# An encoder layer in split float32: the down projection's weights at other byte shifts, in longer tiles

## The chip, the cores and the metric

The kernel runs on one core of one Trainium2 chip. The time is the device time of one execution in microseconds; a kernel's time is the median of its runs. The engines are named as in the profile: PE (TensorE; PEld are its weight loads), ACT (ScalarE), DVE (VectorE), POOL (GpSimd) and SP (SyncE, which here only issues DMAs).

## The reference

One layer over 1024 rows of 1024 float32: pooling and differential attention, merged by gates, then the multi-layer perceptron whose last product is the down projection:

```python
def reference(x, ...):
    ...
    x = x + merged @ w_out[l]
    h2 = rmsnorm(x, g_ffn[l])
    x = x + jnp.square(jax.nn.relu(h2 @ w_up[l])) @ w_down[l]
    return x
```

`h2` is 1024 x 1024, `w_up` 1024 x 4096, `w_down` 4096 x 1024.

## The kernel before

**Digits.** Every float32 operand of a product is split in two: `hi`, a rounded copy of the value, which ACT casts (line 131), and `lo`, what is left, which DVE (or POOL) subtracts (line 132). A product `a b` is then three matmuls into one PSUM bank, `hi hi`, `hi lo` and `lo hi` (`mm3`, lines 137 to 139). In the matmuls of the down projection the stationary operand, which TensorE loads as weights, is a 128 x 128 block of `uh` or `ul` (activation sums), and the moving one is 128 x 512 of `wh` or `wl` (rows of `w_down` or sums of its quarters).

**The up and the down projection** each take seven products of halves instead of eight, by the scheme of Strassen and Winograd. The up projection runs over 16 pairs of column blocks (`up_pair`, p = 0 to 15). Each pair's results and four sums of them are stored to DRAM (`ud`, `udS`), 8 tiles of 128 x 2 x 512 for each of seven names.

**The down projection** runs over the products `"1"`, `"2"`, `"6"`, `"5"`, `"7"`, `"3"`, `"4"` (`d_product`), and in each over `q` = 0 to 7: 56 pairs (j, q). For a pair, `operands(j, q)` loads the raw activation sums `ur` from DRAM (line 1370) and the raw quarter `wd` of `w_down` (line 1333), or makes a sum of quarters on DVE (`T1s`, `T2s`), and splits both. `d_step` then makes 2 x 4 x 3 matmuls into the four banks of the product (`Da` or `Db`; `i` is the half of the tile, `t` the bank). A tile's name has product and pair, as `u1_0h`: product 1, pair 0, hi; the profile's rows leave the product out (`u_0h`). While product 1 runs, `wdt` quarters are loaded as well, for the sums `T1s` (`t1_made`). `x1y` and the like are the results of a product plus the rows of the residual (`with_residual`).

**Buffers.** The pools of this stage lie on the right side of SBUF one behind the other, in the order `pur0` (2 raw tiles for `ur`), `prw0` (2 for `wd`), `puo` (8 tiles for `u` digits, so that four pairs' digits exist at a time), `pur1` (2), `prw1` (4); `pwo`, 8 tiles for `w` digits, lies on the left. They lie where buffers of the up projection lay (`pr1`, `pr20`, `pr21` for raw `w_up`, `e20`, `e21`, `es` for sums), and a tile may be written once the readers of what lay there before are done.

**The order** of instructions on each engine is set by a scheduler when the program is built. It goes by priorities in the order of the code, and by its own estimate of when things are ready; the first three pairs of product 1 are given the priority of the up projection's last pair (`early`), so that their loads and splits mix with it. Each engine's queue runs in order. SP's queue holds the loads of both raw operands, so a load that waits for a buffer holds up all behind it.

Of the kernel before, what the change touches and what calls it, by code (L numbers as in the profile page):

```python
# [9 lines left out]
F32R = mybir.dt.float32r  # L10
# [7 lines left out]
P = 128  # L18
# [37 lines left out]
}  # L56
O_TAIL = "a0 70 n0 71 n1 72 n2 40 s0 n3 73 41 s1 42 t0 s2 43 t1 s3"
A_ROOM = {"1": 1, "2": 0, "6": 1, "5": 0, "3": 1, "7": 0, "4": 1}

N_OP, N_E1, N_E2, N_R1, N_R2 = 8, 11, 6, 4, 3  # L60

# [2 lines left out]
def encoder_kernel(  # L64
# [22 lines left out]
    x, out = x[0], out[0]  # L87
# [41 lines left out]
    def split(hi, lo, src, lo_eng=None):  # L129

        nc.scalar.copy(hi, src)  # L131
        return (lo_eng or nc.vector).tensor_tensor(lo, src, f(hi), op=ALU.subtract)  # L132
# [281 lines left out]
    with ExitStack() as ph:  # L414
# [364 lines left out]
        for g in range(-2, N + 10):  # L779
# [11 lines left out]
            for tok in ORDER:  # L791
                if tok not in gens:
                    i = g - tok[1]
# [66 lines left out]
    for d in range(NK):  # L860
        if d % 2 == 0 and d + 2 < NK:
            ws_bp[d + 2] = load_cols2(w_branch_pool, (d + 2) * P, f"bp{d + 2}")
        elif d > NK - 4:
            j = len(ws_ba)
# [12 lines left out]
    def a_set(j, d):  # L877

        t = hp0[A_ROOM[j]].tile([P, 2, 512], F32R, tag="H", name=f"A{j}_{d}")
        a_sets.setdefault(j, []).append(t)  # L880
# [455 lines left out]
    def second(j, q):  # L1336

        if j == "1":
            b11[q] = quarter(j, q, 0, 0)
            return b11[q]  # L1340
        if j == "5":
            return T1s[q]
        if j == "2":
            return quarter(j, q, 1, 0)
        if j == "3":
            return quarter(j, q, 1, 1)
        if j == "6":
            b22 = quarter(j, q, 1, 1)
            T2s[q] = kept("T2", q)
            sub(dve, T2s[q], b22, T1s[q])  # L1350
            return T2s[q]
        if j == "7":
            b22, b12 = quarter(j, q, 1, 1), quarter(j, q, 0, 1)
            sub(dve, b22, b22, b12)
            return b22
        b21 = quarter(j, q, 1, 0)
        sub(dve, b21, b21, T2s[q])
        return b21
# [8 lines left out]
    def operands(j, q):  # L1367
        nraw[0] += 1
        ur = purs[nraw[0] > 2 and nraw[0] % 2].tile([P, 2, 512], F32, tag="ur", name=f"ur{j}_{q}")
        nc.sync.dma_start(ur, ud[SIDES[j][0], q])  # L1370
        out_ = []
        for n, src, pool_ in (("u", ur, puo), ("w", second(j, q), pwo)):
            hi, lo = (pool_.tile([P, 2, 512], F32R, tag="op", name=f"{n}{j}_{q}{x}") for x in "hl")
            split(hi, lo, src, dve)
            out_ += [hi, lo]
        return out_
# [11 lines left out]
    def d_product(banks, j, last=False, early={}):  # L1388
        for q in range(NQ - 2 if last else NQ):
            d_step(banks, j, q, early.get(q) or operands(j, q), range(4))  # L1390
            if j == "1" and q > 1:
                t1_made(q - 2)
        if j == "1":
            t1_made(NQ - 2)
            t1_made(NQ - 1)
        if last:
            ops = {q: operands(j, q) for q in (NQ - 2, NQ - 1)}
            for t in range(4):
                for q in ops:
                    d_step(banks, j, q, ops[q], (t,))  # L1400
# [23 lines left out]

    now, tc.cur_priority = tc.cur_priority, last_pair
    early = {q: operands("1", q) for q in range(3)}
    tc.cur_priority = now
    DX = four("a")
# [49 lines left out]
```

## Time and profile before

| | |
|---|---|
| median of 3 runs (lowest, highest) | 1532.88 us (1532.23, 1533.74) |
| the profiled execution | 1532.49 us; its span, first to last instruction, 1530.7 us |
| busy, share of the span: PE, PEld, DVE, ACT, POOL | 99%, 86%, 67%, 52%, 25% |
| granted TensorE clock | 1.00 |
| chain that ended last | PE 97%, DVE 2% |
| down projection | from 1221.7 us on, about 309 us |

PE's busy share counts matmuls that overlap each other in the pipeline, so the distance from one start to the next is the better measure of its rate. A row of a timeline has start and length in us, engine, line, operation, tiles, and in brackets the idle time before it and what ended it. A row of a tile has duration in ns (least, median, most) and the first and last start in us.

### The profile page before, as it was taken

To read this page: it belongs to the slowest core of one execution; us is meant where nothing else is said; L and a number is where in the kernel's file an instruction comes from. 1 tells how busy PE (TensorE), PEld (TensorE's weight loads), DVE (VectorE), ACT (ScalarE), POOL (GpSimd) and SP (SyncE) were. 2 spreads that over 40 slices of the span, in tenths; PEclk is the share of its full clock that TensorE was granted. 3 is DMA by queue.
4 is the path that set the end of the run, shared out by engine and by line. 5 is a ranking of instruction groups with operands and counts; after the bars stand their busy time and mean duration, and the time that the engine had idled before them with its cause. 6 is when DMAs were issued, how large, how long until landed. Compare 5 with 4: busy or idle time off the path is not lost.

```text
span 1530.7 us, 21680 instructions
## 1 busy us (share of the span) xinstructions
PE 1513.4 (99%) x7601; PEld 1314.4 (86%) x7601; DVE 1027.9 (67%) x2129; ACT 794.7 (52%) x1650; POOL 390.1 (25%) x469
## 2 busy tenths in 40 slices
PE   7999999999999999999999999999999999999999
PEld 6999999999999999888888887888888788888887
DVE  7777766677777777743654899676656678556572
ACT  5656555555555565544633467565555634333331
POOL 5434242433435352317736610000000000000000
PEclk9999999999999999999999999999999999999999
DMA  7111111111202021329844633555433889537650
GB/s 226 42 58 60 46 56 56 50 56 34 76 33 80 31 90 49 114 99 365 279 148 164 210 149 117 172 186 166 151 124 110 288 322 369 188 124 261 228 192 28
DMA packets 168569, 214.28 MB, mean 140 GB/s; under 512 B 10158, under 2 KB 104075, under 8 KB 168459
## 3 DMA queue, kind: packets, MB, share of 16 engines
q1 hardware_dynamic: 151050, 185.58, 35.8%
q10 hardware_dynamic: 17408, 27.30, 4.9%
q8 instruction: 60, 0.98, 0.3%
q14 instruction: 51, 0.41, 0.1%
HBM read 155.14 MB, written 57.70 MB: 139 GB/s over the span
## 4 chain that ended last, share of the span: by engine, by line
PE 97%; DVE 2%; DMA 0%; issue 0%; ACT 0%; SPq 0%; POOL 0%; ACTq 0%; POOLq 0%
PE z L139 6%; PE z L137 6%; PE z L138 6%; PE g L139 4%; PE g L138 4%; PE g L137 4%; PE Da L138 4%; PE Da L139 4%; PE Da L137 4%; PE Db L137 3%; PE Db L139 3%; PE Db L138 3%; PE X L139 3%; PE X L137 3%; PE X L138 3%; PE sc L630 2%
## 5 line engine op out<-in xcount | busy, mean ns | idle before, releaser
L137 PE MATMUL z<-wqkv,hT 128*128 128x384 f32 x512 | 175.5, 343 | 0.0
L139 PE MATMUL z<-wqkv,hT 128*128 128x384 f32 x512 | 174.3, 341 | 0.7 <-DVE hT L132 0.7
L138 PE MATMUL z<-wqkv,hT 128*128 128x384 f32 x512 | 174.7, 341 | 0.0
L641 ACT ACTIVATE s<-s,nm 128x256 f32<-128x256 f32 (+7 forms) x128 | 99.6, 778 | 74.3 <-DVE nm L633 71.5
L270 POOL TENSOR_TENSOR ms<-ms,mhalf 128x4 f32<-128x4 f32 x64 | 65.1, 1017 | 207.7 <-DVE ms L269 196.5
L137 PE MATMUL g<-hT,fwgate 128*128 128x512 f32 x256 | 101.1, 395 | 0.0
L139 PE MATMUL g<-hT,fwgate 128*128 128x512 f32 x256 | 100.6, 393 | 0.0
L138 PE MATMUL g<-hT,fwgate 128*128 128x512 f32 x256 | 100.5, 393 | 0.0
L137 PEld LDWEIGHTS z<-wqkv,hT 128*128 128x128 f32 x512 | 97.3, 190 | 2.6 <-ACT hT L131 0.4
L139 PEld LDWEIGHTS z<-wqkv,hT 128*128 128x128 f32 x512 | 97.1, 190 | 2.7 <-DVE hT L132 1.5
L138 PEld LDWEIGHTS z<-wqkv,hT 128*128 128x128 f32 x512 | 97.4, 190 | 1.7
L633 DVE CUSTOM_DVE_ANT_0 s<-sc,dist 128x512 f32<-128x512 f32 (+3 forms) x128 | 74.3, 585 | 23.3 <-PE sc L631 22.3
L630 PE MATMUL sc<-K,Q 128*128 128x512 f32 (+2 forms) x192 | 67.2, 355 | 0.4 <-DVE nm L633 0.4
L631 PE MATMUL sc<-K,Q 128*128 128x512 f32 (+2 forms) x192 | 66.3, 349 | 0.0
L132 POOL TENSOR_TENSOR wqkv<-rqkv,wqkv 128x384 fp32r<-128x384 f32 x60 | 62.4, 1055 | 12.9 <-ACT wqkv L131 8.1
L132 DVE TENSOR_TENSOR AS<-s,AS 128x512 fp32r<-128x512 f32 x64 | 43.5, 689 | 32.9 <-ACT AS L131 32.8
L132 POOL TENSOR_TENSOR fwgate<-frgate,fwgate 128x512 fp32r<-128x512 f32 x32 | 44.1, 1378 | 63.5 <-ACT fwgate L131 63.5
L139 PEld LDWEIGHTS g<-hT,fwgate 128*128 128x128 f32 x256 | 48.1, 188 | 9.6
L137 PEld LDWEIGHTS g<-hT,fwgate 128*128 128x128 f32 x256 | 48.2, 188 | 9.0 <-ACT go L388 0.2
L138 PEld LDWEIGHTS g<-hT,fwgate 128*128 128x128 f32 x256 | 48.2, 188 | 8.6 <-issue 0.2
L137 PE MATMUL ba<-yT,wba 128*128 128x512 f32 x128 | 49.7, 389 | 0.0
L139 PE MATMUL ba<-yT,wba 128*128 128x512 f32 x128 | 49.7, 389 | 0.0
(458 smaller groups left out, 4597.9 us busy)
## 6 DMA issues: line engine op xcount, KB each, us to landing
wd<-in_w_down_dram SPq DMA_DIRECT2D x56, 512.0 KB, 5.5
wu<-in_w_up_dram SPq DMA_DIRECT2D x32, 512.0 KB, 4.9
udS<-us SPq DMA_DIRECT2D x64, 256.0 KB, 3.5
ur<-udS SPq DMA_DIRECT2D x32, 512.0 KB, 3.2
rqkv<-in_w_in_dram SPq DMA_DIRECT2D x64, 192.0 KB, 2.8
ur<-ud SPq DMA_DIRECT2D x24, 512.0 KB, 5.4
frgate<-in_w_gate_dram SPq DMA_DIRECT2D x32, 256.0 KB, 2.7
g_dram<-go ACTq DMA_DIRECT2D x32, 256.0 KB, 2.9
```

What stands on the lines that cost most here:

```text
L132: return (lo_eng or nc.vector).tensor_tensor(lo, src, f(hi), op=ALU.subtract)
L137: nc.tensor.matmul(ps, lhs_hi, rhs_hi, start=first, stop=False, **kw)
L138: nc.tensor.matmul(ps, lhs_hi, rhs_lo, start=False, stop=False, **kw)
L139: return nc.tensor.matmul(ps, lhs_lo, rhs_hi, start=False, stop=last, **kw)
L270: nc.gpsimd.tensor_tensor(dst, dst, mhalf[:, :n], op=ALU.pow)
L630: nc.tensor.matmul(dst, Q[:, i, 0, :], rhs, start=True, stop=False)
L631: nc.tensor.matmul(dst, Q[:, i, 1, :], rhs, start=False, stop=True)
L633: nc.vector.tensor_tensor_reduce(out=s[i][:, c : c + w], in0=sc[:, 0:w], in1=dist[:, o0 + c : o0 + c + w], scale=2.0 ** -(h + 1), scalar=B ...
L641: nc.scalar.activation(s[i][:, 0:n], s[i][:, 0:n], AF.Exp, bias=last, scale=-1.0, accum_out=Z[:, i, t : t + 1])
```

## The change

The `u` tiles of the down projection become 64 floats longer, 1088 in place of 1024 for each partition, and the digits lie `o` floats (4 `o` bytes) behind the tile's start. `o` comes from a table with an entry for each pair (j, q), the same for `hi` and `lo`; products are counted as 1 to 7 in it. It has 24 different values: the multiples of 4 from 0 to 60 three times each, and 1, 2, 3, 5, 6, 7, 62 and 63 once each. The `w` tiles stay as they are. So ACT's cast writes, DVE's subtraction reads and writes, and TensorE's weight loads read at shifted addresses; no instruction is added or left out.

```diff
+SHIFT = [4, 56, 40, 12, 16, 0, 32, 24, 40, 28, 12, 52, 24, 48, 44, 16, 63, 6, 60, 60, 4, 8, 20, 8, 20, 48, 5, 28, 40, 52, 44, 4, 1, 36, 36, 52, 36, 7, 44, 48, 56, 12, 0, 2, 0, 3, 16, 62, 32, 56, 24, 28, 32, 8, 20, 60]
...
         for n, src, pool_ in (("u", ur, puo), ("w", second(j, q), pwo)):
-            hi, lo = (pool_.tile([P, 2, 512], F32R, tag="op", name=f"{n}{j}_{q}{x}") for x in "hl")
+            if n == "u":
+                o = SHIFT[8 * (int(j) - 1) + q]
+                hi, lo = (
+                    pool_.tile([P, 2 * 512 + 64], F32R, tag="op", name=f"{n}{j}_{q}{x}")[:, o : o + 2 * 512]
+                    .rearrange("p (i c) -> p i c", i=2)
+                    for x in "hl"
+                )
+            else:
+                hi, lo = (pool_.tile([P, 2, 512], F32R, tag="op", name=f"{n}{j}_{q}{x}") for x in "hl")
             split(hi, lo, src, dve)
```

The 8 tiles of `puo` take 8 x 256 = 2048 bytes of each partition more, and `pur1` and `prw1` behind them lie 2048 bytes lower. Which buffers of the up projection they overlap changes with that, and with it what the first tiles wait for; the scheduler's order changes between the up projection's last pairs and the first pairs of product 6. Ahead of it and from there on the order on every engine is the one of before, but for two operations of DVE that change places in product 6. Lines below the table are numbered 2 higher, those below `operands` 10 higher. Three places of the order are shown in the prediction.

## Prediction

> **What bounds the kernel now.** I read the page's first part and its chain first, then stretches of the down projection, then single rows.
>
> ```profile
> span 1530.7 us, 21680 instructions
> PE 1513.4 (99%) x7601; PEld 1314.4 (86%) x7601; DVE 1027.9 (67%) x2129; ACT 794.7 (52%) x1650; POOL 390.1 (25%) x469
> PE 97%; DVE 2%; DMA 0%; issue 0%; ACT 0%; SPq 0%; POOL 0%; ACTq 0%; POOLq 0%
> 1222.00:1232.00 10.00, 9.87 (x44) 7.83 (x43) 8.74 (x10) 6.13 (x9) 0.00 (x0) 1.00 0.54 205
> 1232.00:1264.00 32.00, 32.00 (x143) 26.51 (x142) 20.67 (x19) 11.59 (x12) 0.00 (x0) 1.00 0.96 350
> 1264.00:1306.00 42.00, 42.00 (x187) 34.80 (x186) 34.53 (x32) 17.83 (x18) 0.00 (x0) 1.00 0.99 370
> 1306.00:1530.00 224.00, 221.03 (x976) 182.77 (x974) 122.22 (x118) 74.06 (x74) 0.00 (x0) 1.00 0.48 166
> ```
>
> TensorE (PE) is the bound: 97% of the chain that ended last. The last four rows cut the down projection into stretches (length, then busy time and count of PE, of the weight loads, of DVE, ACT and POOL, then granted clock, DMA share, GB/s). From 1222 us on PE is busy all through, at a granted clock of 1.00, and only between 1232 and 1306 us is a second resource near its limit: the DMA engines at 0.96 and 0.99. So the change can move the end in two ways: by the time from one matmul to the next in this stage, or by a wait of PE for digits (the hi and lo parts that ACT and DVE make).
>
> **The change, first part: weights at other addresses.** Each of the 56 pairs feeds 2 x 4 x 3 = 24 matmuls, 1344 in all. Three entries of the table are 0, so 53 pairs, 1272 matmuls, get weights from a new address modulo 256 bytes. In the built program of before every matmul operand of this width starts at a multiple of 256 bytes. What a load and a matmul take there:
>
> ```profile
> L137 PEld LDWEIGHTS Da<-w_2h,u_2h x32: 187/188/188, 1232.9 to 1498.8; 128*128 128x128 f32 x32
> L137 PE MATMUL Da<-w_2h,u_2h x32: 388/390/390, 1233.1 to 1499.0; 128*128 128x512 f32 x32
> ```
>
> ```profile
> 1224.72 0.39 PE L139 MATMUL Da<-w_0h,u_0l 128*128 128x512 f32 x1
> ...
> 1227.44 0.39 PE L139 MATMUL Da<-w_0h,u_0l 128*128 128x512 f32 x1
> ...
> 673.86 0.28 PE L138 MATMUL po<-AT_0l,V 128*128 128x256 f32 x1
> ...
> 676.49 0.28 PE L139 MATMUL po<-AT_4h,V 128*128 128x256 f32 x1
> ```
>
> The first two rows give min/median/max in ns. The timeline rows give starts: 12 steps between the first two, 2.72 / 12 = 227 ns for a matmul of 512 columns; 22 steps between the last two, 2.63 / 22 = 120 ns for 256 columns. The 256 columns more cost 107 ns, so 512 columns alone take 214 ns and some 13 ns are left that do not depend on the width. A load shows 188 ns, yet the matmuls of 256 columns, each with a load of its own, come every 120 ns: loads are pipelined, and beside 227 ns at least 107 ns of a load's part stay unused. A load could therefore become longer by some 100 ns before PE felt it. I take 0 for the loads. The bounds come from below and above: the 13 ns could vanish, -1272 x 13 ns = -16.5 us; for a loss the nearest rows are matmuls of the same width that are longer in other stages:
>
> ```profile
> L137 PE MATMUL g<-hT,fwgate 128*128 128x512 f32 x256 | 101.1, 395 | 0.0
> L630 PE MATMUL sc<-K,Q 128*128 128x512 f32 x96 | 39.1, 407 | 0.4 <-DVE nm L633 0.4
> L137 PE MATMUL Da<-w_2h,u_2h 128*128 128x512 f32 x32 | 12.5, 389 | 0.0
> ```
>
> They are 6 and 18 ns above 389: +7.6 and +22.9 us. The value taken is 0 because the row nearest by place, the load itself, has that slack.
>
> [...]
>
> The casts on ACT (1.05 us) and the subtractions on DVE (1.23 us) that write the digits at the new addresses lie beside PE. In the steady part a digit of u is ready 14 to 15 us before its use (u_4h below: cast at 1227.64, used from 1244.0), so a cast that took twice as long would cost nothing; without that cover it would be 1.05 us for a pair.
>
> **Second part: the pools move.** The eight u tiles grow by 256 bytes each, so that the raw buffers behind them lie 2048 bytes lower and the first u tile overlaps a raw buffer of the up projection's last pair (p = 15). The first u digit now waits until DVE has read that buffer. On ACT, around the last pair, before (u1_0h is the first digit of product 1's pair 0):
>
> ```order
> L131 CAST AS4_14_12663<-s4_14_12582 128x512
> L131 CAST u1_0h_12852<-ur1_0_12848 128x1024
> L1233 COPY z5_14_12618<-Z14_12602 128x512
> L131 CAST AS2_15_12699<-s2_15_12694 128x512
> L131 CAST u1_1h_12864<-ur1_1_12860 128x1024
> ```
>
> and in the changed program:
>
> ```order
> L1208 ACTIVATE U2_14_12600<-U2_14_12600 128x512
> L1213 DMA ud12_7_10148<-U3_14_12636 128x512
> L133 CAST u1_0h_12852<-ur1_0_12848 128x1024
> L1209 ACTIVATE U2_14_12600<-U2_14_12600 128x512
> L133 CAST AS4_15_12777<-s4_15_12696 128x512
> L133 CAST u1_1h_12864<-ur1_1_12860 128x1024
> L1230 COPY U2_15_12714<-X15_12539 128x512
> ```
>
> The two casts have moved back past some dozen instructions, into the time just ahead of the down projection, whose start now looks so:
>
> ```profile
> 1197.65 1.05 ACT L131 CAST u_0h<-ur 128x1024 fp32r<-128x1024 f32 x1
> 1209.50 0.63 ACT L1207 ACTIVATE U<-U 128x512 f32<-128x512 f32 x1
> 1215.98 1.05 ACT L131 CAST u_2h<-ur 128x1024 fp32r<-128x1024 f32 x1 [2.08 <-DMA ur<-ud]
> 1218.40 0.59 ACT L1237 COPY U<-X 128x512 f32<-128x512 f32 x1 [0.42 <-PE X L139]
> 1220.60 1.03 ACT L131 CAST w_0h<-wd 128x1024 fp32r<-128x1024 f32 x1
> 1218.21 1.22 DVE L132 TENSOR_TENSOR u_3l<-ur,u_3h 128x1024 fp32r<-128x1024 f32 x1
> 1221.12 0.69 DVE L807 TENSOR_TENSOR U<-Z,U 128x512 f32<-128x512 f32 x1 [0.50 <-PE Z L139]
> 1221.73 1.22 DVE L132 TENSOR_TENSOR w_0l<-wd,w_0h 128x1024 fp32r<-128x1024 f32 x1
> 1200.52 3.22 SPq L1370 DMA_DIRECT2D ur<-ud  x2
> 1221.68 1.20 PE L137 MATMUL Da<-w_0h,u_0h 128*128 128x512 f32 x4 [0.59 <-ACT w_0h L131]
> 1223.00 0.50 PE L138 MATMUL Da<-w_0l,u_0h 128*128 128x512 f32 x1
> ```
>
> Worked through with these durations: u_0h starts at about 1209.5, where Square stood, and ends at 1210.55; u_0l follows on DVE until 1211.8. The load of ur for pair 3 waits for it, so it goes out at 1211.8 and not at 1200.52, and the one for pair 2 lands behind it: u_2h starts at about 1217.3 and not at 1215.98. In the new order u_2h, the copy of U (PE ends X at 1218.40), u_3h (to 1219.95) and two activations stand ahead of w_0h, which ends at 1222.55 and not at 1221.63; DVE does u_3l after two additions, then U, then w_0l, until 1223.95 and not 1222.95. PE's first matmul moves from 1221.68 to 1222.6 and its first with w_0l from 1223.00 to 1223.95: **+1.0 us**. If pair 2 lands as early as now it is +0.3; one more microsecond of landing makes it +2.2.
>
> From there SP's queue, which issues in order, changes too. Before (ur2 belongs to product 2, wd1 to product 1):
>
> ```order
> L1370 DMA ur2_0_13192<-ud12_0_10141 128x1024
> L1333 DMA wd1_4_00_13006<-in_w_down_dram 128x2x512
> L1333 DMA wdt_2_01_13040<-in_w_down_dram 128x2x512
> L1333 DMA wd1_5_00_13046<-in_w_down_dram 128x2x512
> L1333 DMA wdt_3_01_13080<-in_w_down_dram 128x2x512
> L1370 DMA ur2_1_13228<-ud12_1_10142 128x1024
> ```
>
> and after:
>
> ```order
> L1372 DMA ur2_1_13228<-ud12_1_10142 128x1024
> L1335 DMA wd1_4_00_13006<-in_w_down_dram 128x2x512
> L1335 DMA wdt_2_01_13040<-in_w_down_dram 128x2x512
> L1335 DMA wd1_5_00_13046<-in_w_down_dram 128x2x512
> L1335 DMA wdt_3_01_13080<-in_w_down_dram 128x2x512
> L1372 DMA ur2_2_13264<-ud12_2_10143 128x1024
> ```
>
> The load for w_4 now stands behind ur2_1, which waits for DVE's u_5l, and it needs T of pair 0, which DVE does after u_5l:
>
> ```profile
> 1232.50 0.38 SPq L1333 DMA_DIRECT2D wd<-in_w_down_dram  x1
> 1235.43 0.34 SPq L1370 DMA_DIRECT2D ur<-ud  x1
> 1234.17 1.23 DVE L132 TENSOR_TENSOR u_5l<-ur,u_5h 128x1024 fp32r<-128x1024 f32 x1 [0.57 <-ACT u_5h L131]
> 1238.48 1.05 ACT L131 CAST w_4h<-wd 128x1024 fp32r<-128x1024 f32 x1 [4.34 <-DMA wd<-in_w_down_dram]
> 1239.56 1.23 DVE L132 TENSOR_TENSOR w_4l<-wd,w_4h 128x1024 fp32r<-128x1024 f32 x1 [4.17 <-ACT w_4h L131]
> 1227.64 1.05 ACT L131 CAST u_4h<-ur 128x1024 fp32r<-128x1024 f32 x1 [0.57 <-PE Da L138]
> L137 PE MATMUL Da<-w_4h,u_4h x8: 389/390/390, 1244.0 to 1248.8; 128*128 128x512 f32 x8
> 1263.83 1.23 DVE L132 TENSOR_TENSOR w_0l<-wd,w_0h 128x1024 fp32r<-128x1024 f32 x1 [1.24 <-ACT w_0h L131]
> 1264.98 1.28 DVE L807 TENSOR_TENSOR x1y<-Da,x1y 128x512 f32<-128x512 f32 x2
> L138 PE MATMUL Db<-w_0l,u_0h x24: 388/390/390, 1266.7 to 1444.8; 128*128 128x512 f32 x24
> ```
>
> u_5l ends at 1235.4 and T at 1236.6, so w_4's load goes out at 1236.6 and not at 1232.50, 4.1 us later against PE. Today w_4l is done at 1240.8 and needed at about 1244.7: 3.9 us of slack. The load now has one transfer ahead of it and not a full queue, so I expect it after some 4 us and not after the 6.0 us of today (1232.50 to 1238.48): no wait, 0 us (to +0.2 if it takes as long as today). At product 2 there is less: w_0l ends at 1265.1 and is needed at 1266.7, 1.6 us. In DVE's new order three additions x1y stand ahead of w_0l, and the third needs the third bank of product 1, which PE ends 3 x 227 ns = 0.7 us before the product's end. Addition 0.69 and w_0l 1.23 give a w_0l at 1.35 us after that end; PE has 4 x 227 ns = 0.9 us of matmuls that need only w_0h: **+0.5 us** (0 to +2). Later pairs have 4 us and more.
>
> **Sum.** The profiled execution took 1532.49 us, 1.8 us more than its span; +1.0 +0.5 +0 gives 1534.0. The median of the three runs is 0.4 us above that execution: 1534.4 us.
>
> **Rivals.**
> - *Loads from shifted addresses lengthen each matmul (slower).* For it: no row of before tests such an address, and 13 ns per matmul stay unexplained beside the columns. Against it: the 107 ns of slack. Price: 6 ns, as in the gate's matmuls, +7.6 us: 1542.0 us. It decides from 1.2 ns a matmul (1.6 us) on.
> - *Shifted addresses free part of the 13 ns (faster).* For it: that remainder is on the path of every matmul. Against it: it is the same 13 ns at both widths, as a fixed step would be. Half of it: -1272 x 6.5 ns = -8.3 us, 1526.1 us; all of it: 1517.9. [...]
> - *w_0 of product 2 comes late (slower).* The DMA engines are 0.96 busy from 1232 to 1264 us, so 4.1 us lost at the queue may stay lost, and in the new order one more u transfer (512 KB, 1.4 us at 370 GB/s) stands ahead of it. w_0h has 1266.7 - 0.9 - 1263.8 = 2.0 us. Price 4.1 + 1.4 - 2.0 = 3.5 us in place of 0.5: 1537.4 us. It decides once the load is over 2 us late.
>
> **How the numbers follow.** A measurement of this kernel can tell about 0.2%, 3.1 us. The forecast (1533.2 to 1535.9, within that bound) gets 0.45, longer matmuls 0.27, because the new addresses are untested, shorter ones 0.15, late digits 0.13. So faster 0.15, same 0.45, slower 0.27 + 0.13 = 0.40. The range runs from 1526.0, half of the 13 ns freed, to 1542.5, just over the gate's 6 ns; left out are the fuller half of the gain (0.07) and a loss above 6 ns (0.12).
>
> **What would show it.** Right: steps of 227 ns in the down projection for all shifts, loads near 188 ns, PE's first Da matmul about 1 us later, an idle of some 0.5 us before the first w_0l of product 2, and no other. Wrong: steps that differ from pair to pair with the shift, in either direction, or an idle of PE of over 2 us around 1244 or 1267 us.

## The result and the profile after

The changed kernel took 1544.81 us (median of three runs, 1542.64 to 1548.02) against 1532.88 us: a ratio of 1.0080, interval 1.0050 to 1.0109. The forecast was 1534.4 us, its range ended at 1542.5. The profiled execution took 1544.81 us, 12.3 us more than that of before.

The page of after, busy time by engine and the chain by engine:

```profile
span 1543.0 us, 21684 instructions
PE 1519.7 (98%) x7601; PEld 1312.8 (85%) x7601; DVE 1023.4 (66%) x2129; ACT 793.9 (51%) x1650; POOL 391.3 (25%) x469
PE 93%; DVE 2%; DMA 2%; ACT 1%; SPq 1%; issue 1%; POOL 0%; ACTq 0%; DVEq 0%; POOLq 0%
```

PE is still the bound, but ACT, SP's queue and a DMA now stand in the chain: PE waits somewhere. PE has 6.3 us more busy time for the same 7601 matmuls, and the weight loads have no more than before (1312.8 against 1314.4 us): the matmuls became longer.

Where PE waits, by the timeline of after (start, duration, engine, what; idle before it and its releaser). The first three rows are PE's last matmul of the up projection, its first of the down projection and its first of product 2; the last is the cast that the third waits for:

```profile
1220.72 0.39 PE L141 MATMUL Z<-B22h,AS 128*128 128x512 f32 x1
1224.17 1.20 PE L139 MATMUL Da<-w_0h,u_0h 128*128 128x512 f32 x4 [3.07 <-ACT w_0h L133]
1271.66 1.19 PE L139 MATMUL Db<-w_0h,u_0h 128*128 128x512 f32 x4 [2.26 <-ACT w_0h L133]
1270.57 1.04 ACT L133 CAST w_0h<-wd 128x1024 fp32r<-128x1024 f32 x1 [5.92 <-DMA wd<-in_w_down_dram]
```

Before, PE's idle time at the start was 0.59 us and the first Da matmul stood at 1221.68: the start is 2.5 us late. At product 2 there was no wait; now 2.66 us lie between its first matmul and the one before (1269.01, below), where a step is 0.23: 2.4 us.

The same 200 us out of the steady part, before and then after (length, busy time and count of PE, of the loads, of DVE, ACT and POOL, granted clock, DMA share, GB/s):

```profile
1300.00:1500.00 200.00, 200.00 (x884) 165.70 (x883) 118.79 (x113) 72.79 (x74) 0.00 (x0) 1.00 0.55 192
```

```profile
1300.00:1500.00 200.00, 200.00 (x866) 162.17 (x865) 120.55 (x115) 72.01 (x72) 0.00 (x0) 1.00 0.62 205
```

PE is busy all through, at the same clock, with 866 matmuls where there were 884: 200 / 884 = 226 ns for a step, 200 / 866 = 231 ns. Single rows of after, in a pair whose shift is 24, and the group of w_2h, u_2h (min/median/max ns):

```profile
1267.60 0.40 PE L141 MATMUL Da<-w_7h,u_7l 128*128 128x512 f32 x1
...
1269.01 0.40 PE L141 MATMUL Da<-w_7h,u_7l 128*128 128x512 f32 x1
L139 PEld LDWEIGHTS Da<-w_2h,u_2h x32: 187/188/192, 1235.6 to 1510.4; 128*128 128x128 f32 x32
L139 PE MATMUL Da<-w_2h,u_2h x32: 388/394/400, 1235.8 to 1510.6; 128*128 128x512 f32 x32
```

Six steps in 1.41 us are 235 ns. The load keeps its 188 ns (192 at most), the matmul beside it takes 394 ns where it took 390.

The account of the two profiled executions: the down projection starts 2.5 us later, PE waits 2.4 us at product 2, and the rest of the projection grows from 304.96 to 314.77 - 2.43 = 312.34 us between first and last matmul, 7.4 us over the 1272 matmuls with shifted weights or **5.8 ns each**. 2.5 + 2.4 + 7.4 = 12.3 us, the whole difference.

By shift (4-byte elements), the mean steps worked out from the starts: 227.3 ns for 0, 226.7 for 3, 226.8 for 63, 227.9 for 60; 230 to 232 for 1, 2, 6, 20, 44, 48, 52; 233 to 235 for the thirteen others. So it is not the shift's size, and not whether it is a multiple of four. One shift does not always have one price either: of the three pairs shifted by 48, two take 229.3 ns and one 233.3 through all its 24 matmuls; why is not known.

### The profile page after: what moved, and what is told of

It is laid out like the page before. It is cut to its first block, busy times and chain, and to the rows that moved or that the text cites. A ratio compares the mean times of both kernels' runs of the same rounds, so it can differ in the third digit from the quotient of the medians.

```text
span 1543.0 us, 21684 instructions
## 1 busy us (share of the span) xinstructions
PE 1519.7 (98%) x7601; PEld 1312.8 (85%) x7601; DVE 1023.4 (66%) x2129; ACT 793.9 (51%) x1650; POOL 391.3 (25%) x469
## 4 chain that ended last, share of the span: by engine, by line
PE 93%; DVE 2%; DMA 2%; ACT 1%; SPq 1%; issue 1%; POOL 0%; ACTq 0%; DVEq 0%; POOLq 0%
PE z L141 6%; PE z L139 6%; PE z L140 6%; PE g L141 4%; PE g L140 4%; PE g L139 4%; PE Da L140 3%; PE Da L141 3%; PE Da L139 3%; PE Db L140 3%; PE Db L141 3%; PE Db L139 3%; PE X L141 3%; PE X L139 3%; PE X L140 3%; PE sc L632 2%
```

## The experiments

Behind each time stand its ratio to the kernel before, measured beside it (1532.1 to 1533.5 us), and the 95% interval of the ratio.

**Waits and longer matmuls apart.** The long tiles and moved pools alone:

```diff
-SHIFT = [4, 56, 40, 12, ...
+SHIFT = [0] * 56
```

> The long tiles and the moved pools stay, every entry of the table is 0. Theory (two separate costs: late digits from the moved pools, and longer matmuls from the shifted weights): the late start (2.5 us) and the wait at product 2 (2.4 us) stay and all matmul steps of the down projection are 227 ns, so 1532.9 + 4.9 = about 1537.8 us. Rival (the shifts make the waits, or the 4352-byte stride of the tiles lengthens the matmuls): 1533 us in the first case, about 1545 us with steps of 232 ns in the second.

1539.66 us (1.0042, 1.0030 to 1.0054), with 884 matmuls in the 200 us. The order and both waits are those of the changed kernel (idle of 2.23 us at the start and 2.48 us at product 2), the steps are back at 227 ns. So the waits do not come from the shifts, nor the longer steps from the tiles' stride. It is 1.9 us above the expected 1537.8, and the windows of this run show a cost that nobody had expected:

```profile
1222.00:1224.40 2.40, 1.83 (x7) 1.20 (x8) 1.71 (x2) 2.40 (x5) 0.00 (x0) 0.98 0.77 237
1224.40:1228.00 3.60, 3.60 (x11) 2.82 (x10) 3.30 (x4) 2.97 (x5) 0.00 (x0) 0.54 0.59 208
1228.00:1267.90 39.90, 39.90 (x177) 33.01 (x176) 24.99 (x24) 11.28 (x11) 0.00 (x0) 1.00 0.85 293
1267.90:1270.80 2.90, 0.42 (x3) 0.03 (x1) 1.85 (x5) 1.13 (x2) 0.00 (x0) 1.00 1.05 399
1270.80:1272.60 1.80, 1.74 (x5) 1.12 (x6) 1.80 (x2) 1.80 (x3) 0.00 (x0) 0.86 1.06 414
1272.60:1276.00 3.40, 3.40 (x10) 2.69 (x9) 3.40 (x4) 1.91 (x3) 0.00 (x0) 0.57 1.03 388
```

The granted clock falls to half 1.8 us after the end of the first wait and 1.3 us after that of the second, for 3.4 us each time: seven or eight steps of 427 ns, about 1.6 us. (The rows show a little more than 0.5 because their stretches reach beyond it.) The changed kernel's profiled run had no such stretch in spite of its two waits.

The other way round, all shifts but the order of before: the lowest of the eight places of u, which overlaps the raw buffer of the up projection's last pair, is used only for the last digit of every fourth pair.

```diff
-    puo = pool_of(ctx, "puo", 8, side="right")
+    puo = pool_of(ctx, "puo", 7, side="right")
+    pul = pool_of(ctx, "pul", 1, side="right")
...
-    pool_.tile([P, 2 * 512 + 64], ...
+    (pul if q % 4 == 3 and x == "l" else pool_).tile([P, 2 * 512 + 64], ...
```

> All shifts as in the change; the lowest of the eight places, which overlaps the raw buffer of the last pair, is kept for the last digit of every fourth pair, so that the first digit need not wait, and the instructions stand as before but for four loads on SP's queue. Theory of two separate costs: the waits go, the longer steps stay (mean 232.5 ns in the shifted pairs), 1344 x 5.2 ns = 7 us, about 1540 us. Rival (the longer steps only come with the late, crowded order, through the DMA traffic beside them): steps of 227 ns, about 1533 us.

1542.62 us (1.0058, 1.0046 to 1.0070), 865 matmuls in the 200 us. The wait at product 2 is gone: it came from the order that the late first digit brought. (The five other kernels with this order do not have it either, and the run without shifts, with the changed kernel's order, does.) The longer steps stayed. The start was still late (1.85 us of idle), and some 1.6 us went to one stretch at half clock behind it (3.30 us at a granted 0.51). The same kernel with all shifts 0:

> Long tiles, all shifts 0, the lowest place of u kept for the last digit of every fourth pair, the raw buffers of w_down as in the change: the run with the shifts and this layout, without its shifts. Theory (the two costs add: in this layout no wait at product 2 and a start about 1.2 us late, as that run showed; the rest of its time came from the shifts): steps of 227 ns, about 1534 us, and 7 to 8 us below the run with the shifts. Rival (the longer tiles cost by themselves, by the clock or the DMA traffic): 1537 us or more.

1535.06 us (1.0011, 1.0001 to 1.0021), 884 matmuls. Of the 9.2 us of the run before, 7 come from the shifts.

The late start that remains points to a second overlap. The raw buffers of w_down lie behind those of u and move down too; in the built program the buffer of w_down's pair 2 lies over an s tile of pair 15, where before it lay over tiles of pair 14 alone. Two loads on SP's queue, the second of which is this one, and u_2h's cast on ACT, before and then after:

```profile
1195.48 3.41 SPq L1333 DMA_DIRECT2D wd<-in_w_down_dram  x2
```

```profile
1195.49 6.13 SPq L1335 DMA_DIRECT2D wd<-in_w_down_dram  x2
1219.02 1.05 ACT L133 CAST u_2h<-ur 128x1024 fp32r<-128x1024 f32 x1 [4.21 <-DMA ur<-ud]
```

The second load goes out 2.7 us later and SP holds what stands behind it. u_2h's cast starts at 1219.02 and not at 1215.98, but in the changed kernel that load of w_down is not what holds it up. SP's queue further on, before and then after:

```profile
1211.62 0.82 SPq L1370 DMA_DIRECT2D ur<-ud  x2
```

```profile
1203.04 0.47 SPq L1335 DMA_DIRECT2D wdt<-in_w_down_dram  x1
1211.75 0.34 SPq L1372 DMA_DIRECT2D ur<-ud  x1
1212.36 0.34 SPq L1213 DMA_DIRECT2D udS<-us  x1
1212.75 0.94 SPq L1372 DMA_DIRECT2D ur<-ud  x2
```

The loads of ur for pairs 2 and 4 are the last row each time. In after, the load for pair 3 (1211.75) stands ahead of them and waits until u_0l is done; SP had issued nothing for 8 us by then, so the 2.7 us were over. Pair 2's load leaves at 1212.75 where it left at 1211.62, and lands after 6.3 us where it took 4.3. In the run with the lowest place last it leaves in time, but still takes 5.9 us to land.

To take both overlaps away (all shifts 0):

```diff
-    prws.append(pool_of(ctx, "prw1", 4, side="right"))
+    prws.append(pool_of(ctx, "prw1", 3, side="right"))
+    prws.append(pool_of(ctx, "prw2", 1, side="right"))
...
-        r = prws[0 if first else 1].tile(...
+        nraw[2] += not first
+        r = prws[0 if first else 1 + (nraw[2] % 4 == 0)].tile(...
```

> Long tiles, all shifts 0, and both pools that moved (the digits of u, and the raw buffers of w_down below them) use their lowest place for every fourth tile only, so that neither the first digit of u nor the load of w for pair 2 waits for the last pair of the up projection. Theory (the late start and the wait at product 2 come from these two overlaps): the first Da matmul starts about 1 us after the last matmul of the up projection, as before, PE does not wait at product 2, about 1533.5 us. Rival (something else in the longer tiles costs, such as the DMA traffic or the clock): still 1537 us or more.

1537.29 us (1.0030, 1.0020 to 1.0041): half right. PE's first Da matmul:

```profile
1223.99 1.20 PE L139 MATMUL Da<-w_0h,u_0h 128*128 128x512 f32 x4 [0.90 <-ACT w_0h L133]
```

(The up projection itself ended 2.0 us later in this execution than in that of before, so the start is to be read by the idle time.) With both overlaps gone the idle time is 0.90 us here and 0.78 to 1.20 in three more kernels with these places, against 1.55 to 2.93 in six with the first alone removed. So the second overlap has a part in the late start of those six; what it adds in the changed kernel, which has both, was not separated. But PE waits 3 us at product 2: this arrangement changes the order of the w loads of product 1, and w_0 of product 2 comes late again. Which load costs it there was not separated, and it is not the order alone: of the three other kernels with these places and this order two wait there as well (2.7 and 2.0 us), and the one with only the lo digits shifted does not.

**What makes a matmul longer.** With the lowest place last and the weights u at multiples of 256 bytes, the moving operand w shifted by the table:

```diff
-            if n == "u":
-                o = SHIFT[8 * (int(j) - 1) + q]
+            o = SHIFT[8 * (int(j) - 1) + q] if n == "w" else 0
```

> Order as in the run with the lowest place last; the weights u lie at multiples of 256 bytes, and the moving operands w are shifted by the same table in long tiles. Theory A (what counts is where the weights lie): steps of 227 ns everywhere, about 1533 us. Theory B (what counts is the distance between weights and moving operand, modulo 256 bytes): steps near 233 ns in the shifted pairs, about 1540 us. Theory C (any operand off a multiple of 256 bytes costs by itself): also longer, but with other numbers per shift, 1536 to 1545 us.

1541.19 us (1.0051, 1.0039 to 1.0063), 863 matmuls in the 200 us. Weights at their old alignment, and the steps are as long: theory A is out. Then both by the same entry (the condition dropped):

> Order as in the run with the lowest place last; weights and moving operand of a pair are shifted by the same entry of the table. Theory A (weights alone): as with the weights alone shifted, steps near 232.5 ns, about 1540 us. Theory B (distance of the two): back to 227 ns in all pairs, about 1533 us. Theory C (each costs by itself): longer than either alone, 1543 to 1550 us.

1540.44 us (1.0048, 1.0036 to 1.0061), 870 matmuls. None of the three as stated: pairs whose shift is a multiple of 8 elements are back at 227 to 229 ns, odd multiples of 4 stay at 231 to 233. So the distance counts, and something finer beside it. 56 combinations of two shifts in one kernel:

> 56 different pairs of shifts (weights a, moving operand b), in 4-byte elements. Theory B (only the distance a - b modulo 64 elements counts where both are multiples of 8): (64,0), (0,64) and (64,64) take 227 ns; (16,0), (24,8), (32,16), (48,32), (40,24) and (0,48) agree within 1 ns near 233; (48,0), (56,8), (0,16), (8,24), (16,32) agree near 229 to 231. Theory C (each operand costs by its own address): (24,8) and the like differ from (16,0) and come nearer to the sum of two costs, 239 ns.

The kernel took 1545.25 us in one run; its steps are what it was made for. First and last matmul of three of its pairs, with shifts of weights and moving operand of (16,0), (40,24) and (64,0):

```profile
1339.57 0.39 PE L140 MATMUL Da<-w_4h,u_4h 128*128 128x512 f32 x1
...
1344.93 0.39 PE L142 MATMUL Da<-w_4h,u_4l 128*128 128x512 f32 x1
...
1484.15 0.40 PE L140 MATMUL Db<-w_6h,u_6h 128*128 128x512 f32 x1
...
1489.53 0.39 PE L142 MATMUL Db<-w_6h,u_6l 128*128 128x512 f32 x1
...
1423.13 0.39 PE L140 MATMUL Da<-w_3h,u_3h 128*128 128x512 f32 x1
...
1428.36 0.39 PE L142 MATMUL Da<-w_3h,u_3l 128*128 128x512 f32 x1
```

23 steps each: 5.36 / 23 = 233 ns, 5.38 / 23 = 234 ns, 5.23 / 23 = 227 ns. From all starts, for shifts that are multiples of 8 (a - b modulo 64 elements, which are 256 bytes):

| distance | mean step of its pairs, ns |
|---|---|
| 16: (16,0) (24,8) (32,16) (40,24) (48,32) (0,48) | 233.2 232.8 233.8 233.6 232.8 233.0 |
| 32: (32,0) (40,8) (48,16) (16,48) (0,32) | 233.3 232.7 232.4 233.3 232.3 |
| 48: (48,0) (56,8) (0,16) (8,24) (16,32) | 229.3 230.1 229.4 229.8 228.9 |

Theory B holds to about 1 ns, at distances 8, 24 and 56 too (233, 234 and 233 ns); (64,0), (0,64) and (64,64) take 227.3 to 228.6. The shift of 48 in the changed kernel, 229.3 or 233.3 ns, shows that a distance can still have two prices. Where both are odd multiples of 4 the distances have other prices: (20,4) and (28,12), 16 apart, take 229 ns, (12,4) and (20,12), 8 apart, 227 to 228. As a test on whole kernels, both shifted by multiples of 8, at distance 0 and at distance 32:

```diff
+SHIFT = [o // 8 * 8 for o in SHIFT]
...
-            o = SHIFT[8 * (int(j) - 1) + q]
+            o = (SHIFT[8 * (int(j) - 1) + q] + 32 * (n == "w")) % 64
```

The first line alone makes the kernel at distance 0, both make the other.

> The same layout; weights and moving operand of each pair both shifted by the table's entry rounded down to a multiple of 8 elements, so that their distance modulo 64 elements is 0. Theory (the step goes by the distance): 227 to 228 ns, 1534 to 1535 us, as without shifts. Rival (each shift costs by itself): 1540 us and more.

> As the run with equal shifts, but the moving operand 32 elements further (modulo 64), so that the distance is 32 elements in all 56 pairs; tiles, order and the set of addresses are the same. Theory: 232 to 233.5 ns in all 1344 steps, 1344 x 5.8 ns = 7.8 us above the run with equal shifts, about 1542 us. Rival (it is the addresses and not their distance): the same time as that run.

The 200 us at distance 0, then at distance 32:

```profile
1300.00:1500.00 200.00, 200.00 (x880) 164.79 (x879) 119.73 (x114) 73.71 (x74) 0.00 (x0) 1.00 0.58 198
```

```profile
1300.00:1500.00 200.00, 200.00 (x862) 161.82 (x861) 118.72 (x113) 71.03 (x73) 0.00 (x0) 1.00 0.60 202
```

1536.80 us (1.0022, 1.0014 to 1.0031) and 1543.82 us (1.0066, 1.0051 to 1.0082): 7.0 us between two kernels with the same tiles, order and shifts of u, by the distance alone; the mean steps of the two traces, 228.0 and 232.5 ns, make 6.1 us of it. Both lie 2 us above the expected values, the first also 1.7 us above the kernel without shifts. By the starts, steps 10 to 23 of a pair take 226 to 227 ns, the last one, beside which the next pair's weights load from another shift, 231 to 232, and the first nine 228 to 231.

The 53 changes of pair in this trace tell where the price is paid. The first two rows are the last matmul of a pair and the tenth of the next, where the shift goes from 40 to 16; the other two are the same places where it stays at 24:

```profile
1306.73 0.40 PE L142 MATMUL Db<-w_6h,u_6l 128*128 128x512 f32 x1
...
1309.05 0.39 PE L140 MATMUL Db<-w_7h,u_7h 128*128 128x512 f32 x1
...
1416.07 0.39 PE L142 MATMUL Da<-w_2h,u_2l 128*128 128x512 f32 x1
...
1418.33 0.39 PE L140 MATMUL Da<-w_3h,u_3h 128*128 128x512 f32 x1
```

Ten steps take 2.32 us in the first case and 2.26 in the second. At the seven changes to an equal shift nothing happens; at the 46 others the steps around the change are longer, and the sum depends on the distance between the new shift and the old one alone, to 1 ns: 34 ns together at distance 8, 42 at 16, 49 at 24, 10 at 32, 51 at 40, 12 at 48 and 32 at 56. All changes together make 1.5 us of the 1.7. Each matmul's own weights lie at distance 0 from its moving operand here, so the price is paid where a load lies at another distance from the operand that streams just then, and it fades over some ten steps. An earlier run of equal shifts, in the layout with two low places:

> Weights and moving operand of each pair are shifted by the same entry, rounded down to a multiple of 8 elements (32 bytes). Theory B with the parity seen before (equal shifts cost nothing if they are multiples of 32 bytes): all steps near 227 ns and, the places being those of the unshifted run with two low places, about 1533.5 to 1534.5 us. Rival (any shift costs, equal or not): steps of 230 ns and more, 1538 us.

1537.62 us (1.0032, 1.0019 to 1.0046): the steps took 228 ns too, and the time was missed by that layout's 2 us at product 2. Last, only the lo digits of u shifted:

> Only the lo digit of u is shifted by the table; hi digits and w lie at multiples of 256 bytes. Three matmuls follow each other: hi x w hi, hi x w lo, lo x w hi. Theory L (the load of shifted weights gets in the way of the matmul that runs beside it): the step of hi x w lo, beside which the lo digit is loaded, takes 233 to 240 ns, the other two 227 ns. Theory M (a matmul is slow when its own weights lie off the moving operand): the step of lo x w hi is the long one.

1537.04 us in one run, 868 matmuls in the 200 us, and neither theory as stated: over the shifted pairs the three kinds of step took 230.5, 231.6 and 231.6 ns. Behind a change of pair, in the run above, some ten steps share the price (2.32 against 2.26 us), so a disturbed step can also disturb the next, and this run does not tell the two apart. The changes of pair above do: theory M gives them nothing to pay.

## Why the prediction was wrong

- **The loads (taken at 0, measured 7.4 us) are the step that failed most.** The load did not lengthen, as predicted: 188 ns. But the slack of a load says nothing of what the load does to the matmul beside it, and that is where the time went: at distance 0 and at distance 32 a load takes 187.5 and 187.9 ns on average (164.79 us / 879 and 161.82 us / 861), and the kernels lie 7.0 us apart. The rival "longer matmuls" had the price right (6 ns and 7.6 us; measured 5.8 ns and 7.4 us), from the nearest row of the same width; I preferred the argument from slack to it. That the price fits is luck: the gate's operands start at multiples of 256 bytes, like all of this width before, so its longer matmuls have another cause, which was not looked into. No pair's mean step fell under the 226.7 ns of before, so nothing of the 13 ns was freed; that they were "the same at both widths" was no evidence, since they were worked out from just these two widths. The point of "what would show it wrong" was met: steps that differ with the shift.
- **The start (predicted +1.0, at most +2.2; measured +2.5).** The chain by way of the first digit was there (u_0h started at 1209.42, as forecast), but u_2h came at 1219.02 and not at 1217.3. The step that was too small is the load of ur for pair 2: it stands behind pair 3's on SP's queue, left 1.1 us later and took 2.0 us longer to land, where the sum had 1.3 us for both. Why it took longer to land stays open. The other pool that moved, the raw buffers of w_down, had not been looked through; its share here is open too. And the term is no fixed number: with the same order, the run without shifts started 1.6 us late.
- **Product 2 (predicted +0.5; measured +2.4).** The rival "w_0 of product 2 late" happened, at 2.4 us where it was priced 3.5. What was lost at SP's queue was not made up by the shorter DMA queue that the sum for w_4 had counted on: from the issue of w_4's load to its cast passed 5.8 us (1239.24 to 1245.01) where some 4 were expected and 6.0 had passed before.
- **The rivals were weighed as if only one could happen.** Their causes were separate, so their prices add, and the sum of 2.5 + 2.4 + 7.4 us lies beyond a range that ended at the dearest one alone.
- Right were the casts and subtractions at nothing, the move of the order, and w_4's delay. Its load is the first of the two rows of SP's queue in after:

```profile
1239.24 0.38 SPq L1335 DMA_DIRECT2D wd<-in_w_down_dram  x1
1239.68 0.46 SPq L1335 DMA_DIRECT2D wdt<-in_w_down_dram  x1
```

It went out 6.7 us later than before, 4.2 us later measured from the start.

## What to carry to other kernels

In a stream of fp32r matmuls like this one keep weights and moving operand at the same place modulo 256 bytes, in multiples of 32: equal shifts cost 1.3 ns a matmul here, and only where the shift changes; a shift of one cost 5.8 ns on average, 2.6%. It is not the only thing that lengthens a matmul, as the gate's show (395 ns against 389). A tile that grows moves every pool behind it: go through all of them for a new neighbour in the last buffers of the stage before. Where two rivals have separate causes, add their prices.

## What the runs showed beside

In five profiled runs TensorE went at half clock, with steps of 427 ns in place of 227, after PE had stood still for 1.55 to 2.93 us at the start of the down projection; the stretches that were cut out of three of them last some 3.4 us. That of the run without shifts and with the lowest place last, behind an idle time of 2.16 us:

```profile
1223.40:1226.90 3.50, 3.50 (x9) 2.74 (x10) 2.22 (x2) 3.50 (x7) 0.00 (x0) 0.53 0.45 176
```

The five are among eight with an idle time of over 1.5 us there; in the other three (1.64 and 2.03 us, and the changed kernel's 3.07) the steps stayed as they were. What decides between the two is not known. A whole stretch costs about 1.6 us, seven or eight steps of 427 ns in place of 227: a wait of 2 us can cost more than 3.5.
